# Issuing the first two pieces of x from ScalarE's queue instead of the sync engine's, in a two-layer hybrid attention kernel

## The chip, the cores and the metric

The kernel runs on one core of one Trainium2 chip. The metric is device time in microseconds of one execution. The time before is the median of three runs.

## The reference, cut to what matters

Two identical layers are applied to x of shape (1, 256, 1024), in float32. Each projects x with one wide matrix, splits the result into the inputs of three mixers (a gated MLP, a sparse attention with three branches, a memory attention), joins their outputs, projects back and normalises.

```python
def hybrid_layer(x, mem, w_in, ..., w_mem_kv, w_out, ln_g, ln_b):
    h = x @ w_in
    (gm_u, gm_v, gm_z, nq, nkc, nvc, nks, nvs, nkw, nvw, ngate, nz,
     mq, mz) = jnp.split(h, SPLIT_POINTS, axis=-1)
    y_gm = gmlp_mixer(gm_u, gm_v, gm_z, gm_ln_g, gm_ln_b, gm_ws, gm_bs)
    y_nsa = nsa_mixer(nq, nkc, nvc, nks, nvs, nkw, nvw, ngate, nz, ...)
    y_mem = memory_mixer(mq, mz, mem, w_mem_kv)
    y = jnp.concatenate([y_gm, y_nsa, y_mem], axis=-1) @ w_out
    return layer_norm(ALPHA * x + y, ln_g, ln_b)
```

## The kernel before, in words

x is kept transposed as eight pieces ("chunks") of 128 of the 1024 model columns by 256 tokens. A weight tile, for example tile B of the first layer (512 output columns), is likewise loaded as eight chunks of 128 rows; one chunk is 256 KB. Every float32 operand is split into a rounded high part and a low part: ScalarE casts the raw chunk to the high part (`split`, CAST), VectorE subtracts it from the raw chunk to get the low part (TENSOR_TENSOR). A product of two split operands then takes three matmuls (`mm3`: high by high, high by low, low by high). So TensorE can finish chunk k of a projection only when chunk k of x and chunk k of the weight have both been loaded, cast and subtracted.

`load_T` loads x in five DMAs: chunk 0, chunk 1, chunks 2 and 3, chunks 4 and 5, chunks 6 and 7 (128, 128, 256, 256 and 256 KB), all into the buffer `dup`. `eighth` loads one weight chunk. For the eight chunks of tile B of the first layer the raw buffers are, in order, gz, mz, gu, gv, kmr, vmr, qr and nz (the list `EARLY`); buffers of those names hold other things later. Weight chunks after them go to the `wr` ring and to whichever of these buffers are idle. All loads are issued by the sync engine (SP), on one hardware queue.

No instruction is issued where the program text has it. The class `Plan` records every operation, then `schedule` works out an order for all engines together: `pack` is a list scheduler with a table of costs and a model of the DMA path, and around it runs a random walk with a fixed seed that shifts the priorities of some operations, packs again, and keeps what its model finds shorter, for 1000 packings. `emit` issues the operations in the order of the best plan. As every instruction is issued inside `emit`, the profile gives nearly all of them the one line L336, and they are told apart by tile. Operations with a `rank` are taken ahead of all others by the list scheduler: those of x chunk c have rank 2c, those of tile B's chunk k have rank 2k+1, so that x and weight chunks alternate. In `pack` a DMA on the sync engine keeps it for the model's issue time, a DMA on another engine keeps that engine for 500 ns, and both kinds share one modelled issue path and one modelled bus:

```python
if o["dma"]:
    if len(lanes) >= self.DMA_LANES:
        t = max(t, heapq.heappop(lanes))
    hw = max(t, hw) + o["issue"]
    free[e] = hw if e == sync else t + cost
    bus = max(bus, hw + self.DMA_BEFORE) + o["bytes"] / self.DMA_RATE
```

Before the data arrive TensorE runs nine matmuls on zeros (`warm`, written to tile o). `bank` gives projections accumulators of the names acc and o by turns.

Of the kernel before, what the change touches and what calls it, by code (L numbers as in the profile page):

```python
# [339 lines left out]
def hymba_kernel(ctx: ExitStack, tc: tile.TileContext, xT, xN, memT, w512, wC, cw1, par, gln, lngb, const, out):  # L340
    nc = Plan(tc.nc)
# [4 lines left out]
    def buf(tag, shape, dtype=F32, space=sb):  # L346

        if tag not in rings:
            n, size = BUFS.get(tag, (1, 0))
            size = max(size, int(np.prod(shape[1:])))  # L350
            rings[tag] = [0, [space.tile([P, size], dtype, name=f"{tag}{i}") for i in range(n)]]
        ring = rings[tag]
        t = ring[1][ring[0] % len(ring[1])]
        ring[0] += 1
        dims = "abcd"[:len(shape) - 1]
        t = t[:shape[0], :int(np.prod(shape[1:]))]
        return t.rearrange(f"p ({' '.join(dims)}) -> p {' '.join(dims)}", **dict(zip(dims, shape[1:])))
# [13 lines left out]
    def split(h, l, src, eng=None):  # L371
        nc.scalar.copy(h, src)
        (eng or nc.vector).tensor_sub(l, src, h)


    def load_T(src, hl, tag, urgent=False):

        for half in range(2):
            raw = buf(tag, [P, 4, S])
            for k0, k1 in ([(0, 1), (1, 2), (2, 4)], [(0, 2), (2, 4)])[half]:  # L380
                ks = slice(4 * half + k0, 4 * half + k1)
                nc.rank = 2 * ks.start if urgent else None
                nc.sync.dma_start(raw[:, k0:k1], src[:, ks])
                h, l = [t[:, ks] for t in hl]
                if urgent and ks.start in XV:
                    nc.vector.tensor_copy(h, raw[:, k0:k1])
                    nc.vector.tensor_sub(l, raw[:, k0:k1], h)
                else:
                    split(h, l, raw[:, k0:k1])
        nc.rank = None  # L390
# [82 lines left out]
    l = 0  # L473
    x_T = tiles_T("xT", "xT")
    load_T(xT, x_T, "dup", True)
    nc.sync.dma_start(ct, const)

# [70 lines left out]
    for l in range(L):  # L548
# [10 lines left out]
        ks = [buf("ks" + i, [P, 2, 2, S], F32R) for i in "hl"]  # L559
# [316 lines left out]
        def step_M():  # L876
            if l == 0:
                m_T = tiles_T("yT", "mT")
                load_T(memT, m_T, "dup")
                km0 = xn.rearrange("p b d -> p (b d)")[:, :1024].rearrange("p (i c t) -> p i c t", i=2, c=2)  # L880
                mem.append([km0[:, 0], km0[:, 1]])
                mem.append([buf(i, [P, 2, 256]) for i in ("kmr", "vmr")])
                for m in range(2):
                    w = weights(f"M{m}", l)
                    nc.scalar.copy(mem[m][0], projT2(m_T, w, 0).rearrange("p (c t) -> p c t", c=2))
                    for b in range(NB):
                        nc.scalar.mul(mem[m][1][:, b, :], proj(m_T, w, b, 256, 256, bank("acc")[:, :256]), 0.5)
            y_T.extend(tiles_T("yT", "yT"))
# [134 lines left out]
```

## Time and profile before

| what | us |
|---|---|
| median of 3 runs | 296.26 |
| lowest and highest run | 294.97, 296.74 |
| the profiled execution's own time | 295.48 |
| its span in the profile | 293.7 |

The profiled execution lies 0.78 us under the median, and 1.78 us of its time lie around the span. The times in the rows below are microseconds from the start of the span. PE is TensorE's matmul row, PEld its weight loads, DVE VectorE, ACT ScalarE, POOL GpSimd, SP the sync engine and SPq its DMA-issuing instructions. Ends of matmuls are modelled, so that the busy time of PE is read for where it has gaps. The profile has one hardware DMA queue in use by the kernel, the sync engine's.

### The profile page before, as it was taken

Reading aid. Unit: us, or ns where it says so; the run is one execution under the profiler, and the core shown is the slowest. Engines: PE = TensorE matmul, PEld = TensorE weight load, DVE = VectorE, ACT = ScalarE, POOL = GpSimd, SP = SyncE. Lnnn points to the kernel's source line nnn. Section 1 sums busy time; section 2 is a strip of 40 time slices with the busy share of each in tenths; the row PEclk is TensorE's granted clock in tenths of the full one; section 3 lists DMA queues with packets and bytes.
Section 4 is the critical chain, followed back from the end, with each engine's and each line's share of the span. In section 5 each row is a group of like instructions: output and inputs, shape, how many; then the busy total and the mean of one; then the engine's idle time right before and its main releaser. Section 6 shows DMA issues by size and latency. Waiting matters only on the chain.

```text
span 293.7 us, 5787 instructions
## 1 busy us (share of the span) xinstructions
PE 281.6 (96%) x1837; PEld 248.1 (84%) x1837; DVE 266.2 (91%) x662; ACT 224.9 (77%) x537; POOL 64.2 (22%) x89
## 2 busy tenths in 40 slices
PE   8999999999999999999999999999999999899990
PEld 3688899988999899777778888898998899687890
DVE  3889889789979998999999998899899999999985
ACT  4877786888998877999776177689969979989400
POOL 0003029304220435020010100491201146000011
PEclk9999999999999999999999999999999999999996
DMA  6999897597766715677257739847685433300012
GB/s 190 388 389 388 251 264 225 141 265 222 236 159 182 233 39 158 209 232 208 72 161 211 225 97 259 271 136 252 190 233 172 121 134 105 111 36 0 2 71 73
DMA packets 30062, 53.66 MB, mean 183 GB/s; under 512 B 3536, under 2 KB 6352, under 8 KB 29904
## 3 DMA queue, kind: packets, MB, share of 16 engines
q1 hardware_dynamic: 30032, 53.30, 58.6%
q8 instruction: 14, 0.23, 0.3%
q14 instruction: 16, 0.13, 0.2%
HBM read 49.09 MB, written 1.05 MB: 171 GB/s over the span
## 4 chain that ended last, share of the span: by engine, by line
PE 63%; ACT 15%; DVE 12%; DMA 5%; issue 3%; SPq 0%; DVEq 0%; ACTq 0%
PE o L336 31%; PE acc L336 22%; PE tp L336 6%; ACT w L336 5%; PE sc L336 3%; ACT pr L336 3%; DVE w L336 2%; DMA wr<-in_w_dram 2%; DMA dup<-dup 2%; DMA mz<-in_w_dram 1%; ACT dup L336 1%; DVE gv L336 1%; DVE pr L336 1%; ACT pTh L336 1%; ACT csTr L336 1%
## 5 line engine op out<-in xcount | busy, mean ns | idle before, releaser
L336 DVE TENSOR_TENSOR w<-wr,w 128x512 fp32r<-128x512 f32 (+1 forms) x84 | 58.9, 715 | 4.8 <-ACT w L336 4.7
L336 PE MATMUL acc<-w,xTh 128*128 128x512 f32 (+2 forms) x208 | 58.3, 349 | 0.0
L336 ACT CAST w<-wr 128x512 fp32r<-128x512 f32 (+1 forms) x84 | 50.6, 624 | 6.3 <-DMA wr<-in_w_dram 2.2
L336 PE MATMUL o<-xTh,w 128*128 128x256 f32 x224 | 44.6, 284 | 0.1
L336 PE MATMUL acc<-w,yTh 128*128 128x256 f32 (+1 forms) x160 | 44.2, 344 | 0.4 <-ACT yTh L336 0.4
L336 POOL TENSOR_SCALAR pr<-pr,fs 128x256 f32<-128x256 f32 (+1 forms) x36 | 23.9, 674 | 92.6 <-DVE fs L336 52.1
L336 PEld LDWEIGHTS acc<-w,xTh 128*128 128x128 f32 x208 | 36.8, 189 | 5.2 <-ACT w L336 0.3
L336 PEld LDWEIGHTS o<-xTh,w 128*128 128x128 f32 x224 | 35.7, 189 | 0.8 <-DVE yt L336 0.3
L336 PE MATMUL acc<-w,xTl 128*128 128x512 f32 (+2 forms) x104 | 35.7, 349 | 0.0
L336 ACT ACTIVATE pr<-pr,nm 128x128 f32<-128x128 f32 (+1 forms) x64 | 28.7, 451 | 9.0 <-DVE nm L336 8.9
L336 PE MATMUL o<-w,xTh 128*128 128x512 f32 (+2 forms) x112 | 35.1, 374 | 0.4 <-DVE w L336 0.2
L336 PE MATMUL o<-xTl,w 128*128 128x256 f32 x112 | 31.3, 283 | 0.0
L336 PEld LDWEIGHTS acc<-w,yTh 128*128 128x128 f32 x160 | 27.2, 188 | 4.3 <-ACT yTh L336 1.1
L336 POOL TENSOR_TENSOR dup<-pr,pt 64x120 f32<-64x120 f32 x32 | 21.8, 692 | 37.2 <-ACT pr L336 30.6
L336 PE MATMUL acc<-w,yTl 128*128 128x512 f32 (+1 forms) x80 | 27.1, 347 | 0.1
L336 PEld LDWEIGHTS o<-w,xTh 128*128 128x128 f32 x112 | 20.1, 189 | 5.2 <-DVE w L336 1.2
L336 DVE TENSOR_TENSOR pTl<-tp,pTh 128x512 fp32r<-128x512 f32 x32 | 21.4, 678 | 0.6 <-ACT pTh L336 0.4
L336 PE MATMUL tp<-ct,pr 128*128 128x128 f32 x128 | 21.7, 275 | 0.2 <-DVE pr L336 0.2
L336 PEld LDWEIGHTS acc<-w,xTl 128*128 128x128 f32 x104 | 19.5, 188 | 2.3
L336 PEld LDWEIGHTS o<-xTl,w 128*128 128x128 f32 x112 | 20.9, 188 | 0.3
L336 ACT CAST pTh<-tp 128x512 fp32r<-128x512 f32 x32 | 18.4, 586 | 3.0 <-PE tp L336 1.7
L336 PE MATMUL o<-w,xTl 128*128 128x512 f32 (+2 forms) x56 | 20.5, 366 | 0.0
(202 smaller groups left out, 705.2 us busy)
## 6 DMA issues: line engine op xcount, KB each, us to landing
wr<-in_w_dram SPq DMA_DIRECT2D x69, 256.0 KB, 3.4
gz<-in_w_dram SPq DMA_DIRECT2D x14, 256.0 KB, 2.9
mz<-in_w_dram SPq DMA_DIRECT2D x14, 256.0 KB, 3.6
gu<-in_w_dram SPq DMA_DIRECT2D x8, 256.0 KB, 4.0
wr<-in_cw_dram SPq DMA_DIRECT2D x8, 256.0 KB, 3.6
dup<-in_lngb_dram SPq DMA_DIRECT2D x4, 512.0 KB, 5.3
wr<-in_wC_dram SPq DMA_DIRECT2D x7, 268.0 KB, 5.7
gv<-in_w_dram SPq DMA_DIRECT2D x7, 256.0 KB, 3.5
```

The lines of the kernel that those rows point to most:

```text
L336: getattr(o["eng"].engine, o["op"])(*o["args"], **o["kw"])
```

## The change

The two DMAs that load chunk 0 and chunk 1 of x are recorded on ScalarE, so ScalarE's instruction stream issues them on its own queue. The other three DMAs of x stay with the sync engine. Ranks, casts, subtractions and buffers are unchanged. The first operation of the sync engine is then the load of weight chunk 0. The plan is worked out anew, with the same seed.

```diff
@@ in load_T
                 ks = slice(4 * half + k0, 4 * half + k1)
                 nc.rank = 2 * ks.start if urgent else None
-                nc.sync.dma_start(raw[:, k0:k1], src[:, ks])
+                (nc.scalar if urgent and ks.start < 2 else nc.sync).dma_start(raw[:, k0:k1], src[:, ks])
                 h, l = [t[:, ks] for t in hl]
```

## Rows read from the trace of the kernel before

**Rows 1.** The page, busy time and share of the span of each engine.

```profile
span 293.7 us, 5787 instructions
PE 281.6 (96%) x1837; PEld 248.1 (84%) x1837; DVE 266.2 (91%) x662; ACT 224.9 (77%) x537; POOL 64.2 (22%) x89
```

**Rows 2.** Four stretches: length; PE, PEld, DVE, ACT, POOL busy; clock; DMA share; GB/s.

```profile
0.00:8.00 8.00, 6.39 (x17) 2.88 (x18) 2.42 (x5) 3.56 (x6) 0.38 (x6) 1.00 0.66 203
8.00:40.00 32.00, 31.72 (x176) 26.63 (x175) 29.03 (x51) 26.08 (x51) 3.37 (x3) 1.00 0.99 345
40.00:280.00 240.00, 237.21 (x1597) 212.49 (x1597) 225.50 (x587) 195.15 (x482) 58.50 (x78) 1.00 0.56 166
280.00:294.00 14.00, 6.32 (x54) 6.11 (x52) 9.29 (x21) 0.09 (x1) 1.96 (x2) 0.82 0.21 76
```

**Rows 3.** The chain that ended last, first 25 us: start, length, what.

```profile
2.10 4.05 DMA mz<-in_w_dram
6.18 0.63 ACT w L336
6.83 0.70 DVE w L336
7.58 0.74 PE o L336 x2
...
24.65 6.52 DMA wr<-in_w_dram
```

**Rows 4.** Timeline of the sync engine's queue: start, length, what it issues.

```profile
0.72 0.39 SPq L336 DMA_DIRECT2D dup<-in_xT_dram  x1
1.17 0.41 SPq L336 DMA_DIRECT2D gz<-in_w_dram  x1
1.64 0.42 SPq L336 DMA_DIRECT2D dup<-in_xT_dram  x1
2.10 0.43 SPq L336 DMA_DIRECT2D mz<-in_w_dram  x1
2.58 0.43 SPq L336 DMA_DIRECT2D dup<-in_xT_dram  x1
...
6.17 0.55 SPq L336 DMA_DIRECT2D qr<-in_w_dram  x1
7.77 0.33 SPq L336 DMA_DIRECT2D nz<-in_w_dram  x1
```

**Rows 5.** Timeline of ScalarE: start, length, what; in brackets the idle time before.

```profile
0.72 1.28 ACT L336 ACT_TABLE_LOAD   x1 [0.72 <-PEq L1012]
3.53 0.41 ACT L336 CAST xTh<-dup 128x256 fp32r<-128x256 f32 x1 [1.53 <-DMA dup<-in_xT_dram]
4.13 0.62 ACT L336 CAST w<-gz 128x512 fp32r<-128x512 f32 x1 [0.20 <-DMA gz<-in_w_dram]
...
6.18 0.62 ACT L336 CAST w<-mz 128x512 fp32r<-128x512 f32 x1 [1.00 <-DMA mz<-in_w_dram]
```

**Rows 6.** Stretches of 1 us, columns as in Rows 2.

```profile
1.00:2.00 1.00, 0.83 (x3) 0.28 (x4) 0.12 (x1) 1.00 (x1) 0.00 (x0) 1.00 0.15 37
2.00:3.00 1.00, 1.00 (x4) 0.45 (x3) 0.00 (x0) 0.00 (x0) 0.00 (x0) 1.00 0.65 192
3.00:4.00 1.00, 1.00 (x4) 0.30 (x3) 0.04 (x1) 0.41 (x1) 0.00 (x0) 1.00 1.00 294
4.00:5.00 1.00, 1.00 (x4) 0.35 (x3) 0.61 (x2) 0.84 (x2) 0.00 (x0) 1.00 0.88 264
5.00:6.00 1.00, 1.00 (x4) 0.74 (x4) 0.81 (x2) 0.18 (x1) 0.00 (x0) 1.00 0.77 240
9.00:10.00 1.00, 1.00 (x5) 0.42 (x4) 0.98 (x3) 0.87 (x3) 0.00 (x0) 1.00 1.05 399
```

**Rows 7.** Stretches of 20 us, the extremes of twelve from 40 to 280 us.

```profile
160.00:180.00 20.00, 20.00 (x99) 16.40 (x98) 18.97 (x38) 10.19 (x22) 0.99 (x1) 1.00 0.63 183
...
240.00:260.00 20.00, 19.11 (x140) 17.10 (x138) 19.23 (x57) 19.16 (x51) 6.94 (x8) 1.00 0.30 92
```

## The prediction

> **What bounds the kernel now.** I read the busy times first, then the four large stretches, then the start alone, since only the start is edited. TensorE is the busiest engine, busy for 281.6 of 293.7 us, with VectorE at 266.2 [rows 1]. The stretches show where the missing 12.1 us of TensorE are: 1.6 in the first 8 us (8 less 6.39), 0.3 from 8 to 40 us, 2.8 from 40 to 280 us, and the rest, about 7.4 of 13.7, behind the last matmuls, where the final normalisation and the store run [rows 2]. So from 8 us on TensorE is nearly without gaps to the tail, and a change at the start can be worth only the time by which it lets that unbroken run begin earlier, at most the time before it.
>
> What the run's beginning waits for is shown by the chain that ended last. It goes through the load of weight chunk 1 (into mz), issued at 2.10 and landed at 6.15, its cast to 6.81, its subtraction to 7.53, and TensorE from 7.58 [rows 3]. ScalarE had been idle 1.00 us when that cast began [rows 5], so it was the data that came late, not the engine. The queue of the sync engine shows why the issue was at 2.10: it is the fourth of a row of issues that begin 0.45 to 0.48 us apart, x chunk 0, weight 0, x chunk 1, weight 1 [rows 4].
>
> **The change part by part.**
>
> The issues on the sync engine. Two are taken out in front of weight chunk 1. If the steps stay as they are, weight 0 goes out at 0.72 instead of 1.17, weight 1 at 1.17 instead of 2.10, and x chunks 2 and 3 at 1.64 instead of 2.58 [rows 4]; everything behind moves by about 0.94 us as well, until the queue waits for earlier transfers. That is the upper end of the gain: 2.10 - 1.17 = 0.93 us. x chunk 1 goes out at about 1.17 instead of 1.64 and chunk 0 at 0.72 as now, if ScalarE issues as the sync engine does.
>
> The transfers. An earlier issue is an earlier landing only if the DMA engines are free to take it. x chunk 0 needed 3.53 - 0.72 = 2.81 us from issue to the cast that waited for it, weight chunk 1 needed 4.05 [rows 3 to 5]: 1.24 us of that look like waiting behind others. The stretches of 1 us bear it out: the engines' busy share is 0.15 and 0.65 in the second and third us, then 1.00, 0.88 and 0.77, and 1.05 later, at 37, 192, 294, 264, 240 and 399 GB/s [rows 6]. From 2 to 6 us the share left over is 0.35 + 0.00 + 0.12 + 0.23 = 0.70 us. If it were already full the gain would be 0.00, the lower end. Free engine time of 0.70 us is not all usable, since a transfer needs time before its bytes flow: with the first issue at 0.72, the stretch from 1 to 2 us still has 37 GB/s [rows 4, 6]. I take 0.5 us, half way between 0.00 and 0.93 and under 0.70; both ends stay for the range.
>
> On this point a page speaks against the change. The rows above show engines mostly busy from 3 us on. The Trainium skill, "DMA: Bandwidth & Descriptors", section "Issuing engines are not separate DMA queues", says that DMAs from several engines end up on the same 16 DMA engines and that issuing from several saves only the issuing sequencer's time, which is usually small; by it the sum would lie between the same two ends, and nearer to 0. The trace agrees so far as it has only 0.70 us of share to spare.
>
> x chunk 0 gets company. Before it had the engines to itself for the 0.45 us until weight 0 was issued; after, both queues send at 0.72. If they share evenly, the 128 KB of chunk 0 land when 256 KB have moved, that is 128 KB later, at the 240 to 294 GB/s of the rows 0.45 to 0.55 us [rows 6]. Its cast then runs at about 4.0 instead of 3.53, weight 0's at 4.45 instead of 4.13, chunk 1's at about 5.1, to 5.5. I cost this at nothing: it is hidden by ScalarE's 1.00 us of idle time before weight 1's cast [rows 5], so that cast still can begin at 5.65, 0.5 us earlier than now. Were that cover gone, the 0.5 us gained would be lost again, which is the lower end already named.
>
> The issues on ScalarE. Two DMA instructions are added to its stream. No row shows ScalarE issuing; the nearest are the sync engine's, 0.39 to 0.43 us each at steps of up to 0.48 [rows 4]. ScalarE has one table load of 1.28 us at 0.72 and then sits idle 1.53 us for x chunk 0 [rows 5]. Two issues cost at most 2 x 0.48 = 0.96 us and fit into the 1.53, in whichever order they stand with the table load, so ScalarE's own time costs nothing; queued behind them is only the cast of x chunk 0, which waits for their data anyway. If the issue itself were twice as slow there, 0.4 us of it would show, inside the bounds already kept.
>
> A second hardware queue. No row shows what its use costs outside the span. The nearest number is the 1.78 us around the span with one queue; a second could add between nothing and as much again. It could hardly take anything away, since the first queue stays in use. I take nothing, and 1.8 as the far end.
>
> Behind the first 8 us. From weight 6 (qr, 6.17) to weight 7 (nz, 7.77) the steps of the sync engine's queue grow to 1.6 us [rows 4]: its later issues wait, for earlier transfers and then for free buffers. The chain meets the loads again at 24.65, where 6.52 us go by for one load [rows 3]. The engines are full from 9 us on [rows 6], so the load stream as a whole is earlier by what the start has filled, about the same 0.5 us as TensorE's; neither runs ahead of the other. TensorE is without gaps there [rows 2], hence I let the 0.5 us pass through to the end. What is late next, once weight 1 comes earlier, is x chunks 2 and 3 with weights 2 and 3, all moved by the same amount.
>
> The new order. The edit moves planned times, the random walk decides by planned times, so that from its first differing decision the whole order of 5787 instructions can come out otherwise. What this may cost is bounded by TensorE's gaps. From 40 to 280 us they sum to 2.79 us now (240.00 - 237.21) [rows 2]. No order can win more than these there: -2.8. Among the twelve stretches of 20 us the best has no gap and the worst has 0.89 [rows 7]; if all twelve came out like the worst, the gaps were 10.7, that is +7.9. Nearest is the present state itself, since search, model and number of tries are the same: I take 0, and keep -2.8 and +7.9.
>
> **The sum.** Against the profiled execution: 295.48 - 0.5 + 0 + 0 = 295.0. That execution was 0.78 us under the median of the runs, so against the median 296.26 - 0.5 = 295.8. A measurement of this kernel can tell about 1% from no change, 3.0 us; the whole prize at the start, 0.93 us, is a third of that.
>
> **The rivals.**
>
> A, the forecast: the run begins 0.5 us earlier and the new order is worth about the old one. 295.8, by the ends of the terms and the spread of the runs 294.3 to 297.3. For it speaks that TensorE has few gaps to win or to lose.
>
> B, the gain is hidden or the edit does not do what it says: ScalarE runs its table load first. Then x chunk 0 is issued at 2.00 instead of 0.72 and lands at 2.00 + 2.81 = 4.81. ScalarE casts in order, 0.41 + 0.62 + 0.41 for chunk 0, weight 0 and chunk 1 (the size of chunk 0), and reaches weight 1 at 6.25 [rows 5], where it stands now at 6.18: no gain, 296.3. The same follows if both queues' issues share one path and stretch each other. In its favour: the table load starts at the same 0.72 as the first issue. Against it: the table load needs to stand only ahead of the first cast. A sentence on a price that only a page has: the Trainium skill, "ScalarE: Activation LUTs", section "What ACT_TABLE_LOAD costs", has about 1.38 us of draining behind the 1283 ns of the load; by that weight 1's cast would begin at about 7.6 and the time be 297.7, still inside 1%, while the row shows only the 1.28.
>
> C, slower: the new order is poorer. The place is the stretches in which VectorE is as busy as TensorE (19.23 against 19.11 us in 240 to 260 us [rows 7]): there an order that puts a weight's subtraction ahead of a softmax's step lets TensorE wait. It decides from the point where the added gaps exceed the 0.5 us gained. Half way to all twelve stretches like the worst is +3.9, so 296.26 - 0.5 + 3.9 = 299.7. For it: gaps have more room to grow (7.9) than to shrink (2.8). Against it: the same search with the same model found the present order.
>
> D, faster: the new order closes the gaps that are left. 296.26 - 0.5 - 2.8 = 293.0, if it closes all of them, which is why its chance is small.
>
> **How the numbers follow.** Chances: A 0.58, B 0.12, C 0.18, D 0.12. The time is that of A, 295.8. A and B lie within 1% of 296.26 (293.3 to 299.2): 0.70. C is slower by over 1%, 0.18, and D faster, 0.12. A range from 293.4 to 299.4 holds A and B, the 1.8 us of a second queue, and the nearer parts of C and D; it leaves out less than 2 in 10.
>
> **What would show it.** In the changed profile a second hardware queue should carry two transfers of x; ScalarE should issue them at 0.72 and about 1.2, ahead of or around the table load; the sync engine's first issue should be weight 0 at 0.72 and its second weight 1 near 1.2. The cast of weight 1 should begin near 5.65 instead of 6.18, and TensorE's unbroken run near 7.1 instead of 7.58. TensorE's gaps from 40 to 280 us tell A from C and D: near 2.8 for A, 6 or more for C, under 1 for D. If the start is 0.5 us earlier and the end is not, the order gave it back. The prediction is wrong if the gaps of the middle move by over 3 us, or if ScalarE's queue delivers x so late that the run begins later than 7.58.

## The result, and the profile after

| what | before | after |
|---|---|---|
| median of 8 runs, us | 294.99 | 298.39 |
| lowest and highest, us | 294.01, 296.74 | 297.50, 301.07 |
| the profiled execution's span, us | 293.7 | 296.6 |

The changed kernel is slower: the ratio is 1.0125, with a 95% interval from 1.0099 to 1.0151. The time lies inside the predicted range; the forecast itself, a small gain, has the wrong sign. The medians are 3.4 us apart, the two profiled executions 2.9 us. The median before is now 1.3 us under the 296.26 that the forecast started from, so the forecast's gain of 0.5 us stands for 294.5 here. One disturbed execution, of the changed kernel with another seed further down, is left out of that kernel's figures.

The page of the changed kernel, busy times and hardware queues (packets, MB, share of 16 engines):

```profile
PE 281.7 (95%) x1837; PEld 249.5 (84%) x1837; DVE 265.8 (90%) x662; ACT 223.2 (75%) x537; POOL 66.2 (22%) x89
q1 hardware_dynamic: 29744, 53.04, 57.3%
q10 hardware_dynamic: 288, 0.26, 0.4%
```

TensorE's busy time is the same as before (281.7 against 281.6 [rows 1]), so by this count the 2.9 us are gaps. The count cannot tell a slow matmul from a fast one, which matters below. The second queue is there, q10, with two loads of 0.13 MB in 288 packets: 0.9 KB a packet, where q1's mean is 1.8 KB.

Four stretches of the changed kernel, columns as in [rows 2]:

```profile
0.00:8.00 8.00, 4.79 (x11) 1.71 (x12) 1.91 (x5) 3.44 (x6) 0.38 (x6) 1.00 0.67 227
8.00:40.00 32.00, 32.00 (x169) 27.45 (x168) 27.88 (x50) 23.81 (x49) 5.67 (x3) 1.00 0.97 341
40.00:280.00 240.00, 236.58 (x1594) 212.34 (x1593) 225.17 (x586) 195.37 (x483) 58.15 (x79) 1.00 0.55 166
280.00:297.00 17.00, 8.31 (x70) 8.04 (x68) 10.85 (x24) 0.62 (x1) 1.96 (x2) 0.80 0.17 62
```

Set against [rows 2], the gaps change as follows: 3.21 - 1.61 = +1.60 us in the first 8 us, 0.00 - 0.28 = -0.28 to 40 us, 3.42 - 2.79 = +0.63 to 280 us, and (16.6 - 8.31) - (13.7 - 6.32) = +0.91 at the end. With 0.04 us more of work that is the 2.90 us of the span. Over half of the loss is made where a gain was forecast, before 8 us.

The sync engine's queue of the changed kernel, start, length, what:

```profile
0.72 0.38 SPq L336 DMA_DIRECT2D gz<-in_w_dram  x1
1.17 0.42 SPq L336 DMA_DIRECT2D mz<-in_w_dram  x1
...
4.54 0.33 SPq L336 DMA_DIRECT2D kmr<-in_w_dram  x1
...
6.25 0.33 SPq L336 DMA_DIRECT2D dup<-in_xT_dram  x1
```

ScalarE of the changed kernel, with its queue's two issues in one row:

```profile
0.72 0.89 ACTq L336 DMA_DIRECT2D dup<-in_xT_dram  x2
1.64 1.28 ACT L336 ACT_TABLE_LOAD   x1 [1.64 <-PEq L1012]
4.54 0.41 ACT L336 CAST xTh<-dup 128x256 fp32r<-128x256 f32 x1 [1.62 <-DMA dup<-in_xT_dram]
6.25 0.40 ACT L336 CAST xTh<-dup 128x256 fp32r<-128x256 f32 x1 [1.30 <-DMA dup<-in_xT_dram]
6.56 0.61 ACT L336 CAST w<-gz 128x512 fp32r<-128x512 f32 x1
```

The first issues went as forecast on both engines: weight 1 leaves at 1.17 instead of 2.10 [rows 4], ScalarE issues at 0.72 and 1.15 ahead of its table load. The landings did not. x chunk 0 is cast at 4.54 instead of 3.53, chunk 1 at 6.25 instead of 4.77, where it stood right behind weight 0 [rows 5]. Two lines of the kernel before, of the sync engine and of ScalarE:

```profile
4.48 0.43 SPq L336 DMA_DIRECT2D kmr<-in_w_dram  x1
4.77 0.41 ACT L336 CAST xTh<-dup 128x256 fp32r<-128x256 f32 x1
```

The late x also holds up the sync engine. By the table of waits its queue waits twice for x, 1.9 us together: its seventh load (kmr) goes out at 4.54, when x chunk 0 has landed, and its ninth at 6.25, when chunk 1 has. Before, they went out at 4.48 and 5.58, so the 0.94 us that the later loads were to gain are lost there.

And the order has changed: ScalarE casts chunk 0, chunk 1, weight 0, weight 1, where it was chunk 0, weight 0, chunk 1, weight 1. Weight 0 has landed 3.6 us after its issue at 0.72, but its cast now stands behind the wait for chunk 1, and with it TensorE, as the chain that ended last shows:

```profile
1.15 5.08 DMA dup<-in_xT_dram
...
6.25 0.40 ACT xTh L336
6.66 0.53 ACT w L336
...
7.23 0.80 PE acc L336
```

A load of 128 KB takes 5.08 us and is the first long link, in the place of weight 1's 4.05 us [rows 3].

The wait costs TensorE more than its length. TensorE in the changed kernel, then in the kernel before:

```profile
7.23 0.80 PE L336 MATMUL acc<-w,xTh 128*128 128x512 f32 x1 [2.04 <-ACT w L336]
7.82 0.63 PE L336 MATMUL o<-w,xTh 128*128 128x512 f32 x1
8.25 0.63 PE L336 MATMUL acc<-w,xTh 128*128 128x512 f32 x1
...
10.38 0.63 PE L336 MATMUL o<-w,xTh 128*128 128x512 f32 x2
10.85 0.40 PE L336 MATMUL o<-w,xTl 128*128 128x512 f32 x1
```

```profile
4.80 0.82 PE L336 MATMUL o<-w,xTh 128*128 128x512 f32 x1
...
6.00 0.40 PE L336 MATMUL o<-w,xTh 128*128 128x512 f32 x1
6.24 0.40 PE L336 MATMUL o<-w,xTl 128*128 128x512 f32 x1
```

The matmuls on zeros end at 5.19 in both. In the kernel before data follow without a gap. In the changed kernel TensorE then stands idle for 2.04 us, and from 7.82 to 10.38 its matmuls of 512 columns begin 0.43 us apart; behind that, and in the kernel before from 6.00 on, they begin 0.23 to 0.24 us apart. 512 columns in 0.43 us are the lower of TensorE's two clock levels, 1.2 GHz; 0.23 us lies near the upper, 2.4 GHz. The column of the granted clock has 1.00 in both kernels up to 280 us and does not show it. By an estimate the six steps, 2.56 us, would have taken 1.4 us at 0.23 us each, so the lower level costs about 1.2 us here.

### The profile page after: what moved, and what is told of

It reads as the page before. It is cut to its first block, busy times and chain, and to the rows that moved or that the text cites. A ratio compares the mean times of both kernels' runs of the same rounds, so it can differ in the third digit from the quotient of the medians.

```text
span 296.6 us, 5777 instructions
## 1 busy us (share of the span) xinstructions
PE 281.7 (95%) x1837; PEld 249.5 (84%) x1837; DVE 265.8 (90%) x662; ACT 223.2 (75%) x537; POOL 66.2 (22%) x89
## 4 chain that ended last, share of the span: by engine, by line
PE 71%; ACT 10%; DVE 9%; DMA 5%; issue 3%; SPq 0%; ACTq 0%; DVEq 0%
PE o L336 30%; PE acc L336 30%; PE tp L336 8%; PE sc L336 4%; ACT w L336 3%; ACT pr L336 3%; ACT pTh L336 2%; DMA nz<-in_w_dram 2%; DMA dup<-in_xT_dram 2%; DVE w L336 2%; DMA gz<-in_w_dram 1%; DVE pTl L336 1%; DVE pr L336 1%; ACT csTr L336 1%; DVE xn L336 1%
## 5 line engine op out<-in xcount | busy, mean ns | idle before, releaser
L336 PE MATMUL acc<-w,xTh 128*128 128x512 f32 (+2 forms) x208 | 58.9, 352 | 2.1 <-ACT w L336 2.0
L336 DVE TENSOR_TENSOR w<-wr,w 128x512 fp32r<-128x512 f32 (+1 forms) x84 | 57.3, 703 | 2.9 <-ACT w L336 2.3
L336 ACT CAST w<-wr 128x512 fp32r<-128x512 f32 (+1 forms) x84 | 50.0, 620 | 7.3 <-PE o L336 3.2
L336 PE MATMUL o<-xTh,w 128*128 128x256 f32 x224 | 45.6, 285 | 0.0
L336 PE MATMUL acc<-w,yTh 128*128 128x512 f32 (+1 forms) x160 | 43.7, 344 | 0.3 <-ACT yTh L336 0.3
L336 PE MATMUL acc<-w,xTl 128*128 128x512 f32 (+2 forms) x104 | 36.4, 350 | 0.0
L336 PEld LDWEIGHTS acc<-w,yTh 128*128 128x128 f32 x160 | 27.9, 189 | 3.8 <-ACT yTh L336 0.7
L336 PE MATMUL acc<-w,yTl 128*128 128x256 f32 (+1 forms) x80 | 27.3, 348 | 0.0
L336 PE MATMUL tp<-ct,pr 128*128 128x128 f32 x128 | 23.3, 273 | 1.0 <-DVE yTl L336 1.0
L336 DVE CUSTOM_DVE_ANT_0 pr<-sc,ct 128x128 f32<-128x128 f32 (+1 forms) x64 | 20.5, 346 | 0.9 <-PE sc L336 0.8
```

The costliest lines, as they stand in the source:

```text
L336: getattr(o["eng"].engine, o["op"])(*o["args"], **o["kw"])
```

## The experiments

Theory: two things came with the edit. The x queue gets less than its share of the DMA engines, so that x is late, and a cast that stands in order behind the late x turns this into an idle TensorE. And the plan was drawn anew, and the new order is poorer. Rivals: the order alone, or the queue alone. The diffs show only the lines that matter; those that mark operations are left out, and comments are added.

**The queue alone.** Plan and order of the kernel before; only at emission the first two loads of x (marked "x" when recorded) go to ScalarE.

```diff
-            getattr(o["eng"].engine, o["op"])(*o["args"], **o["kw"])
+            getattr((self.scalar if "x" in o else o["eng"]).engine, o["op"])(*o["args"], **o["kw"])
```

> Every engine keeps the order of the kernel before; only the queue of the first two x loads changes. Theory (share): two queues take turns on the DMA engines, and the x queue, with two loads against up to eight of the sync engine's, gets less than its half, so x chunk 0 lands at about 4.5 and chunk 1 at about 6.2 as in the changed kernel; ScalarE casts in order, weight 1's cast begins near 6.7 instead of 6.18, TensorE has done fewer matmuls by 8 us, and the span grows by 0.3 to 0.8 us, which makes 295.3 to 295.8 against 295.0. Rival (order alone): the queue costs nothing, x lands as before and the time is that of the kernel before or up to 0.9 us less.

Measured: 294.50 against 294.92, ratio 0.9970, interval 0.9945 to 0.9994. The queue alone is a small gain, 0.2 to 1.6 us. ScalarE of this run:

```profile
4.69 0.40 ACT L336 CAST xTh<-dup 128x256 fp32r<-128x256 f32 x1 [1.76 <-DMA dup<-in_xT_dram]
5.00 0.61 ACT L336 CAST w<-gz 128x512 fp32r<-128x512 f32 x1
6.14 0.41 ACT L336 CAST xTh<-dup 128x256 fp32r<-128x256 f32 x1 [0.53 <-DMA dup<-in_xT_dram]
6.46 0.62 ACT L336 CAST w<-mz 128x512 fp32r<-128x512 f32 x1
```

x is as late as in the changed kernel (4.69 and 6.14), which the share theory had said, but the cost it put on this did not come. Weight 0's cast goes ahead of the wait, at 5.00. Weight 1's is 0.28 us later than before, so by 8 us TensorE is a little behind. Two stretches of this run show where it catches up:

```profile
0.00:8.00 8.00, 6.12 (x16) 2.50 (x17) 2.51 (x5) 3.42 (x6) 0.38 (x6) 1.00 0.69 221
8.00:40.00 32.00, 32.00 (x180) 27.51 (x181) 29.42 (x51) 26.54 (x53) 3.40 (x3) 1.00 1.00 350
```

One matmul fewer than [rows 2] by 8 us, four more from there to 40 us, without the 0.28 us of gaps; the last matmul starts at 285.24 instead of 286.04. This gain is not made at weight 1's cast. The loads behind the first ones land earlier: by about 0.2 us from weight 4 on (kmr at 10.38 instead of 10.59), and by about 0.9 us from a load issued near 21 us on, which took 5.8 us instead of 7.3. Whether this second part belongs to the edit, one execution of each kernel does not say.

**The order alone.** Plan and order of the changed kernel; at emission the two loads go back to the sync engine, as its first two.

```diff
+            getattr((self.sync if "x" in o else o["eng"]).engine, o["op"])(*o["args"], **o["kw"])
```

> Every engine keeps the order of the changed kernel; the first two x loads are issued by the sync engine again, as its first two. Theory (both): x chunk 1 lands before 5, the first matmul on data runs near 5.5 instead of 7.23, and about 1.6 us of the 2.9 us come back, the other 1.3 us stay with the order: about 296.3 to 297. Rival (order alone): nothing comes back, 298. Rival (queue alone): all comes back, 295.

Measured: 297.32 against 294.92, ratio 1.0076, interval 1.0047 to 1.0105. ScalarE of this run, behind the cast of chunk 0 at 3.11:

```profile
4.26 0.40 ACT L336 CAST xTh<-dup 128x256 fp32r<-128x256 f32 x1 [0.75 <-DMA dup<-in_xT_dram]
5.22 0.62 ACT L336 CAST w<-gz 128x512 fp32r<-128x512 f32 x1 [0.56 <-DMA gz<-in_w_dram]
```

The same cast order, but chunk 1 has landed by 4.26 and holds up nothing. With one queue this order costs 0.0076 x 294.9 = 2.2 us, more than the 1.3 expected. With this order the queue costs 1.0125 - 1.0076 = 0.5% more (0.4% by the medians, and each ratio has an interval of about 0.3% to either side); with the old order it brought 0.3%. So neither rival stands: the same late x is a loss or none, by what stands behind it.

The 2.2 us are not the price of the changed kernel's order as such, since this run has a late start of its own. Both loads of x go out first, weight 0 is third, at 1.63, and its cast runs at 5.22 instead of 4.13 [rows 5]. TensorE of this run:

```profile
5.89 0.80 PE L336 MATMUL acc<-w,xTh 128*128 128x512 f32 x1 [0.70 <-ACT w L336]
6.49 0.63 PE L336 MATMUL o<-w,xTh 128*128 128x512 f32 x1
```

From 6.49 to 10.33 there are nine steps of 0.43 us, the lower clock level again: an estimate of 3.84 - 9 x 0.23 = 1.8 us. A part of it is made up later: the last matmul starts at 286.71, 0.67 us later than before, and 0.7 us more pass behind it. The queue alone, with 0.48 us of idle time, and the next run, with 0.38, have no such step on data. Idle time does not decide alone: with chunk 1 alone on ScalarE's queue (below) TensorE was idle for 1.11 us without one, and there the last three matmuls on zeros took 1.27 us instead of 1.49, so that the clock had risen before. No run shows what decides it.

With two queues the price of the order is the step from the queue alone to the changed kernel, which differ in nothing else: 1.0125 / 0.9970, 1.55% or about 4.6 us (3.9 us by the medians), each ratio taken against the kernel before of its own series.

**Weight 0's cast ahead of chunk 1's.** The changed kernel, two queues, with two instructions moved.

```diff
+        order = self.schedule()
+        for x, w in zip(self.mark["x"], self.mark["w"]):   # cast, subtraction of x chunk 1; of weight 0
+            order.remove(x)
+            order.insert(order.index(w) + 1, x)
```

> The changed kernel with two queues and its own order, except that the cast and the subtraction of x chunk 1 stand behind those of weight 0 on ScalarE and VectorE. Theory (in-order wait): what made the late chunk 1 cost 1.5 us is that weight 0's cast stands behind chunk 1's cast; moved ahead of it, the first matmul on data runs near 5.7 instead of 7.23 and the time falls by 0.7 to 1.5 us to about 297. Rival: the late chunk alone costs it; the first matmul moves but the time stays at 298.4.

Measured: 296.69 against 295.03, ratio 1.0057, interval 1.0037 to 1.0078. ScalarE, then TensorE:

```profile
4.91 0.61 ACT L342 CAST w<-gz 128x512 fp32r<-128x512 f32 x1
6.23 0.41 ACT L342 CAST xTh<-dup 128x256 fp32r<-128x256 f32 x1 [0.71 <-DMA dup<-in_xT_dram]
...
5.57 0.50 PE L342 MATMUL acc<-w,xTh 128*128 128x512 f32 x1 [0.38 <-ACT w L342]
```

Chunk 1 lands at 6.23 as in the changed kernel, and TensorE starts on data at 5.57 instead of 7.23. Of the 1.25% more than half is gone, 0.68%. The in-order wait is shown, together with what it does to TensorE: there is no step of 0.43 us on data here. What is left, 0.57%, I put down to the rest of the order, less the queue's gain. In the profiled execution, 0.6 us faster than this run's median, the last matmul starts at 285.94, against 286.04 before and 288.03 in the changed kernel, and what is left lies behind it: 8.4 us to the end instead of 7.7.

**The share of the x queue.** Both with plan and order of the kernel before. First, chunks 0 and 1 as one load, whose rows are 2 KB long as the weights' are, where those of one chunk are 1 KB:

```diff
+                if k == 0:
+                    self.scalar.engine.dma_start(raw[:, 0:2], src[:, 0:2])
```

> Order of the kernel before; ScalarE issues chunks 0 and 1 as one load of 256 KB, whose rows are 2 KB like those of the weights, in place of two loads with rows of 1 KB. Theory (share by packets): the engines give each queue one packet in turn, so rows twice as long give x half instead of a third, and 256 KB of x have landed when 512 KB have moved: cast of chunk 0 and 1 near 4.8 to 5.2. Rival (the ScalarE queue is slow or late by itself): the last of x lands at 6.2 again. Time 294.5 to 295.3 by the theory, 295.5 to 296 by the rival.

Then four loads with rows of 512 bytes:

```diff
+                for t in range(0, S, 128):
+                    self.scalar.engine.dma_start(raw[:, k:k + 1, t:t + 128], src[:, k:k + 1, t:t + 128])
```

> Order of the kernel before; ScalarE issues chunks 0 and 1 as four loads with rows of 512 bytes. Theory (share by packets): x gets a fifth, its 256 KB are complete when nearly 1.3 MB have moved, chunk 1 is cast after 7, and the time is 296 to 297. Rival (share by bytes or by load, or a slow queue): chunk 1 lands near 6.2 as with rows of 1 KB, time as with those.

The two queues from 3 to 4 us (packets, MB, share), with rows of 1 KB (the queue alone), 2 KB and 512 bytes in turn:

```profile
q1 hardware_dynamic: 107, 0.19, 51.3%
q10 hardware_dynamic: 99, 0.09, 28.4%
```

```profile
q10 hardware_dynamic: 66, 0.14, 62.0%
q1 hardware_dynamic: 65, 0.12, 37.8%
```

```profile
q1 hardware_dynamic: 166, 0.31, 80.7%
q10 hardware_dynamic: 133, 0.06, 20.6%
```

In each of the three the queues move about as many packets, 99 to 107, 66 to 65, 133 to 166, while the bytes of x are a half, all and a fifth of those of the sync engine. Turns by packet would give that, and a packet is here one row: the 288 of the two loads are 256 rows and 32 small ones. The Trainium skill, "DMA: Bandwidth & Descriptors", section "Queues, rings and completion order", has each DMA engine go round the queues it has work for, one packet at a time, a packet there being several descriptors; the equal counts agree. So x chunk 1's rows of 1 KB against 2 KB are a part of why it took 5.08 us. They are not all of it: as one load with rows of 2 KB, x had landed at 5.54, 0.6 us earlier than chunk 1 of the queue alone (6.12), where chunk 1 of the kernel before was cast at 4.77. The rest is that x shares with the sync engine's loads at all.

The times of these two runs do not follow from the share. The one load had landed when its cast began at 5.56, between what theory and rival had said, and the time was 296.52, ratio 1.0047 (1.0020 to 1.0074): chunk 0's cast now waits for both chunks, weight 0's cast stands behind it at 5.87, and the first matmul on data runs at 6.54 instead of 4.80. It is the in-order wait again, with 1.35 us of idle time and six more steps of 0.43 us. With 512 bytes the time was 298.64, ratio 1.0119 (1.0077 to 1.0161). That run had a second change that I had not meant:

```profile
5.32 1.28 ACT L341 ACT_TABLE_LOAD   x1 [5.32 <-DMA dup<-in_xT_dram]
6.62 0.40 ACT L341 CAST xTh<-dup 128x256 fp32r<-128x256 f32 x1
```

The table load stands behind a wait for x and is no longer hidden: its 1.28 us lie between the landing of x and the first cast. So its time says nothing on the share. When chunk 1 landed is hidden behind it on ScalarE, but the chain that ended last shows it, at 2.13 + 4.89 = 7.02:

```profile
2.13 4.89 DMA dup<-in_xT_dram
```

That is the "after 7" of the theory, not the 6.2 of the rival.

**One chunk only.** Order of the kernel before, chunk 1 alone on ScalarE's queue.

```diff
+            getattr((self.scalar if "x" in o and o["x"][0] == 1 else o["eng"]).engine, o["op"])(*o["args"], **o["kw"])
```

> Order of the kernel before; only x chunk 1 is issued by ScalarE, at 0.72; the sync engine issues chunk 0, weight 0, weight 1 and so on. Theory (share): ScalarE's queue has one load of 128 KB against few of the sync engine's, both chunks land near 3.7 to 4.5, weight 1 goes out at 1.64 and its cast begins near 5.7 instead of 6.18: 0.3 to 0.6 us under the kernel before, as good as both chunks on ScalarE (294.5) or better. Rival (any x on the second queue is late): chunk 1 lands after 5.5 and the time is 294.5 to 295.

Measured: 295.33 against 295.03, ratio 1.0017, interval 0.9990 to 1.0043, no difference. Chunk 0, sharing with chunk 1, is cast at 4.61, weight 0 at 5.41 as soon as it lands, and weight 1 at 6.24, not 5.7: earlier issue did not make weight 1 earlier here either. Neither theory nor rival gave this time a reason; the version with both chunks and the old order stays the better one.

**Where the order costs.** One queue, one part of the operations in one plan's order and the rest in the other's, with the seam at 110 us of planned time.

```diff
+        head = [o for o in new if (o["t"]) < 110000.0]          # the other run: old first, then new
+        done = {o["i"] for o in head}
+        order = head + [o for o in old if o["i"] not in done]
```

> One queue, as before. All operations that the changed kernel's plan starts in its first 110 us come in that plan's order, all others in the order of the kernel before. If the price of the new order (about 2.4 us with one queue) is paid in the first 110 us, this runs near 297; if it is paid behind, where TensorE has 1.1 us more gaps from 120 to 180 us, near 295.5 to 296. The seam may add some of its own.

> One queue. All operations that the plan of the kernel before starts in its first 110 us come in its order, all others in the order of the changed kernel. If the price is paid behind 110 us, near 296 to 297; if in front, near 295. The seam may add some of its own.

Measured: new then old 296.37, ratio 1.0059 (1.0035 to 1.0083); old then new 297.81, ratio 1.0100 (1.0070 to 1.0130). The two add up to 1.6%, twice the 0.76% of the whole order. Either the seam costs by itself, or a loss in one half is made up in the other; no run tells which, and this does not divide the price. One place is seen in the trace. From 120 to 140 us, the changed kernel, new then old, old then new:

```profile
120.00:140.00 20.00, 18.53 (x108) 14.80 (x107) 19.72 (x63) 17.91 (x49) 2.24 (x3) 1.00 0.66 213
```

```profile
120.00:140.00 20.00, 19.63 (x115) 15.66 (x113) 19.48 (x63) 18.31 (x50) 3.16 (x4) 1.00 0.65 209
```

```profile
120.00:140.00 20.00, 18.38 (x107) 14.73 (x105) 19.80 (x64) 17.91 (x49) 2.24 (x3) 1.00 0.64 218
```

TensorE has about 1.5 us of gaps there where the second half is in the new order, and 0.4 where it is in the old. In the changed kernel the longest waits behind the start are, from the table of waits (total, times, longest):

```profile
PE tp L336 <- DVE yTl L336: 1.0, 1, 1.0
PE sc L336 <- DVE cs L336: 1.0, 1, 1.0
```

Both, at 126.98 and 255.15, are TensorE waiting for VectorE, as rival C had it.

**Other draws of the plan.** The kernel before and the changed kernel with another seed of the random walk.

```diff
-    ROUNDS, TRIES, SEED = 8, 1000, 3
+    ROUNDS, TRIES, SEED = 8, 1000, 1      # and 2
```

> The kernel before with another seed of the plan's random walk (1 for 3), nothing else. Theory (a new plan is a draw): the two plans of the kernel before with other seeds lie 1 to 4 us over 295, as the changed kernel's order did with one queue (297.3). Rival (plans are all alike, and the changed kernel's order is poor because of what the edit tells the planner): 294.5 to 295.5.

> The kernel before with seed 2. As with seed 1: 296 to 299 if a new plan is a draw, 294.5 to 295.5 if plans are all alike.

> The changed kernel with seed 1; its plan too puts x chunk 1's cast ahead of weight 0's. Theory: a draw like the kernel before with seed 1, plus about 1.5 us for that cast's place: 297 to 300. Rival (plans alike): 298.4 again.

> The changed kernel with seed 2; its plan too puts x chunk 1's cast ahead of weight 0's. Theory: a draw like the kernel before with seed 2, plus about 1.5 us for that cast's place: 297 to 300. Rival (plans alike): 298.4 again.

Measured, ratios to the kernel before with its own seed:

| seed | kernel before | changed kernel |
|---|---|---|
| 1 | 1.0201 (1.0157 to 1.0246), 300.73 us | 1.0206 (1.0155 to 1.0257), 301.59 us |
| 2 | 1.0162 (1.0140 to 1.0184), 299.84 us | 1.0160 (1.0134 to 1.0186), 299.87 us |

A new plan of the unchanged kernel costs 1.6 to 2.0%, 4.8 and 5.7 us, which is beyond the 1 to 4 us expected. With either seed the edit makes no difference that can be told. With seed 2 the 1.5 us that I had put on the cast's place did not show on top: TensorE begins on data at 6.96 instead of 4.75, and the time is the same, so other gaps cover it. With seed 1 the intervals, 0.5% to either side, could hide it. Stretches of the kernel before with seed 1:

```profile
8.00:40.00 32.00, 30.87 (x173) 26.36 (x172) 29.42 (x51) 26.15 (x51) 1.74 (x2) 1.00 1.02 355
...
120.00:140.00 20.00, 16.57 (x90) 12.88 (x90) 18.17 (x54) 18.05 (x48) 2.02 (x3) 1.00 0.73 229
```

Gaps of 1.1 us and of 3.4 us, where the kernel before has 0.28 [rows 2] and 0.46: 3.8 of the 7.0 us between the two spans are gaps of the order in these two stretches, from an edit of one digit.

## Why the prediction was wrong, point by point

- **What bounds the kernel.** Right that TensorE does; wrong that the start is worth only the time by which the unbroken run begins earlier. The run did begin earlier, at 7.23 instead of 7.58, and my sign of being wrong, a run later than 7.58, did not come. But before 7.58 TensorE had already done six matmuls on data, from 4.80 on, and the changed kernel had done none when its run began. And I took TensorE to run at one speed: about 1.2 us went at the lower clock level behind the idle time, which no term of the sum held.
- **The issues.** Right for the first loads on both engines, 1.17 for weight 1 and 0.43 us steps on ScalarE, its table load hidden. Wrong from the sync engine's seventh load on, which waited for the late x.
- **The transfers, 0.5 us of gain.** For the queue alone the sign is right and the size within what was measured, 0.2 to 1.6 us, but that is luck, since the path was another. I had weight 1's cast at 5.65 and TensorE's run from 7.1; with the old order it was 6.46, later than the 6.18 before, and the gain came with later loads.
- **"x chunk 0 gets company. I cost this at nothing."** This step failed. I gave x an even share, where it got a third of the bytes, since the queues move equal numbers of packets and x's rows are half as long as the weights'. I had chunk 1 cast at about 5.1, where it landed at 6.23. And I named as the cover ScalarE's 1.00 us of idle time before weight 1's cast, with the cast order of the kernel before. In the new order chunk 1's cast stands in front of weight 0's, and the wait for it is TensorE's. Measured price within that order: 0.5% by the two queues set against one (1.0125 and 1.0076), 0.7% by moving the two instructions back (1.0125 and 1.0057), half-speed matmuls included.
- **"The new order. I take 0."** This step failed most. The order of the changed kernel costs 1.55% with two queues, set against the old order with two queues; the 0.7% of the two instructions are a part of it. With one queue it costs 0.76%, 2.2 us, a late start included, and the other redrawn plans 1.6 to 2.0%. I argued that the same search with the same model would find an equal. It found none in any of the draws measured: all of them were slower. The kernel before's plan is the best of those seen, not the usual; no run says whether its seed had been picked for that. The end of the range, +7.9, held; the value taken inside it did not.
- **A second hardware queue's price outside the span.** Right: 298.4 less 296.6 is 1.8 us, as before.
- **Rivals.** C, the poorer order, came in part: TensorE waits for VectorE at two places from 120 us on. But C was to show in the gaps from 40 to 280 us, 6 us or more, and there they are 3.42, near the 2.8 of A; 1.6 us were lost before 8 us and 0.9 us at the end. In the kernel before with seeds 1 and 2 these gaps are 7.0 and 6.3 us, C's size. B's table load stood behind the issues and did no harm, and the 1.38 us of draining that B mentioned were not seen: with rows of 512 bytes, where the load is not hidden, the cast began 0.02 us behind its end. What no rival had is the two together, a late transfer in front of an in-order queue.

What stays open is which of the other moved operations cost the rest of the order's price, 0.57% with the cast's place put right.

## What to carry to other kernels

Where a planner orders the work anew after every edit, measure the edit with the old order first: here the edit was a gain of 0.3% in the old order and a loss of 1.25% in a new one, and a change of the seed alone cost 1.6 to 2.0%. A load on a second queue competed here with all that the first queue had issued, packet by packet, so a small urgent load with short rows came late; rows as long as the others' made it less late, not punctual. Put no other work behind its wait on an in-order engine. And do not price a wait of TensorE at its length alone: look at the steps of its matmuls behind it.

## What the runs showed of the hardware that had not been expected

Two queues with rows of 1 KB and 2 KB moved 99 and 107 packets in the same microsecond, and so a third and two thirds of the bytes. After 2.04 us of idle time TensorE's matmuls of 512 columns began 0.43 us apart for 2.6 us, then 0.23, while the granted clock stood at 1.00. ScalarE's table load was issued in front of the first cast in the runs where that waits for one load, at 1.64 in the changed kernel, and behind the wait, at 5.32, in the one run where the cast's data came in two loads. The last store of the output took 2.6 to 2.8 us to land in the three executions that are wholly in the changed kernel's order, against 2.0 in the kernel before and the others that end in the old order; no run here says why.
